# Two-layer decoder trunk on one core: moving operands placed elsewhere in the partition

## The chip, the cores and the metric

The kernel runs on one core of one Trainium2 chip. The metric is the device time of one execution in microseconds (us), the median of the runs shown. A core has a matrix engine (TensorE, PE in the profile, with its weight load PEld), a vector engine (VectorE, DVE), a scalar engine (ScalarE, ACT), GpSimd (POOL) and a queue engine that only issues transfers (SyncE, SP).

## The reference, cut to what matters

The input has 256 positions of width 1024, in float32. Layer 0 is: half-step SwiGLU, a Mamba-2 mixer, half-step SwiGLU. Then K and V are projected once from the stream. Layer 1 is: half-step SwiGLU, windowed attention over that K and V, half-step SwiGLU; a last RMSNorm ends it.

```python
def swiglu(h, w_gate, w_up, w_down):
    return (jax.nn.silu(h @ w_gate) * (h @ w_up)) @ w_down
...
        x = x + 0.5 * swiglu(rmsnorm(x, norm_w[layer, 0]), ...)      # 1024 -> 2816 -> 1024
        h = rmsnorm(x, norm_w[layer, 1])
        x = x + mamba2_mixer(h, ...)       # layer 0: 1024 -> 5152, scan, 2048 -> 1024
        x = x + swa_sink_attention(h, ...) # layer 1: 16 query heads, 4 key heads
        x = x + 0.5 * swiglu(rmsnorm(x, norm_w[layer, 2]), ...)
```

## The kernel before, in words

Everything is transposed: features lie on the 128 partitions, the 256 positions along them. The stream is eight tiles `X[k]` of 128 x 256. All weights come as 341 units of 128 x 1024 in one written-out order (`ORDER`), two units a transfer on SP's queue, into four buffers `raw`. To keep float32 accuracy each unit is split: ACT writes a rounded `hi` (L144), VectorE the rest `lo` (L155), each in a ring of six tiles of 4,096 bytes. An activation is split likewise, and a product is three matmuls: high by `hi`, low by `hi`, high by `lo`. Each matmul loads 128 x 128 of a weight unit (PEld) and streams the activation, the moving operand, past it.

There are two kinds of products.

- Products of the normed input. The input's parts stand joint in eight tiles `xs[k]` of 128 x 512: high in the first 256 columns, low in the other 256. Gate and up of a feed-forward go through `wide` (L351): for each k one matmul of 512 columns (`hi` by both parts) and one of 256 (`lo` by the high part); with `by_part` the eight of 512 come first and then the eight of 256. `by_part` holds in the two middle feed-forwards for all f but the first. The mixer's input projections and the queries go through `unit` (L336): 24 matmuls of 256 columns, from the same `xs`.
- The second products, through `rows` (L369): down projections (`da`, moving operands `hh`, `hl`), the mixer's output (`sa`, `yh`, `yl`) and the attention's output (`aa`, `oh`, `ol`). A unit is 24 matmuls of 256 columns: three for each of eight output tiles.

There are four feed-forwards of 22 steps f, each step a gate, an up and (four steps late, `LAG`) a down unit. The work between matmuls hangs on the units: after each one `tick` runs what is due in that slot (`Slots`) and splits weights ahead (`ahead`).

Memory of a partition is handed out in pools that stand in the order in which they are opened, each tile padded to 32 bytes. Before the change the order from below is: `const` (sm 2,048 bytes, co 1,024, `X` 8,192, `xs` 16,384, `ones` 512, three small tiles of 32, norms 256), `work` (8,384 in all), `raw` (32,768), `parts` (12 x 4,096: `hi`, then `lo`), and above them the pools of the stages, one after another at the same place (`ffn0`, `ssm`, then `kv` with `ffn1` and `att` above it, `ffn2`). The moving operands of the second products are in the stage's pool: `hh` and `hl` six tiles each, `yh` and `yl` six, `oh` and `ol` four. A tile of a ring is written again only when its last reader is done; a tile of a later pool waits for whatever had its bytes before.

Of the kernel before, what the change touches and what calls it, by code (L numbers as in the profile page):

```python
# [10 lines left out]
F32R = mybir.dt.float32r  # L11
# [5 lines left out]
P = 128  # L17
T = 256
D = 1024
KT = D // P  # L20
NF = 2816 // P
LAG = 4
# [87 lines left out]
class Weights:  # L110


    def __init__(self, nc, w, raw, parts):
        self.nc, self.w, self.raw, self.parts = nc, w, raw, parts
        self.loaded = 0
        self.cut = 0
        self.rounded = 0
        self.pos = 0
        self.chunks = {}
        self.ready = {}  # L120
# [95 lines left out]
class Trunk:  # L216
    def __init__(self, ctx, tc, a):
        self.ctx, self.tc, self.nc, self.a = ctx, tc, tc.nc, a
        nc = self.nc
        self.NPART = 6  # L220
        cp = self.cp = ctx.enter_context(tc.tile_pool(name="const", bufs=1))
        self.wk = ctx.enter_context(tc.tile_pool(name="work", bufs=2))
        raw = ctx.enter_context(tc.tile_pool(name="raw", bufs=RAW))
        parts = ctx.enter_context(tc.tile_pool(name="parts", bufs=self.NPART))
        self.ps = ctx.enter_context(tc.tile_pool(name="ps", bufs=4, space=PSUM))
        self.W = Weights(nc, a["w"], raw, parts)

        self.sm = cp.tile([P, NSM], F32, name="sm")
        self.co = cp.tile([P, NCO], F32, name="co")
        xp = [cp.tile([P, 2, T], F32, name=f"X{k}") for k in range(KT // 2)]  # L230
        self.X = [xp[k // 2][:, k % 2] for k in range(KT)]

        self.xs = [cp.tile([P, 2 * T], F32R, name=f"xs{k}") for k in range(KT)]
        self.xh = [x[:, 0:T] for x in self.xs]
        self.xl = [x[:, T:] for x in self.xs]
        self.ones = cp.tile([P, P], F32, name="ones")
        nc.vector.memset(self.ones, 1.0)
        self.mhalf = cp.tile([P, 2], F32, name="mhalf")
        nc.gpsimd.memset(self.mhalf, -0.5)
        self.eps = cp.tile([P, 1], F32, name="eps")  # L240
        nc.gpsimd.memset(self.eps, EPS)
        warm = cp.tile([P, 1], F32, name="warm")
        nc.scalar.activation(warm, self.ones[:, 0:1], AF.Silu)

        def first(t):
            q, h = nc.sync.dma_start, D // 2
            q(self.norms, a["norms"])
            q(xp[0], a["x"][:, 0:2, :])
            q(t[:, 0, :h], a["w"][0, :, 0, :h])
            q(xp[1], a["x"][:, 2:4, :])  # L250
            q(xp[2], a["x"][:, 4:6, :])
            q(t[:, 0, h:], a["w"][0, :, 0, h:])
            q(xp[3], a["x"][:, 6:8, :])
            for i in range(1, CH):
                q(t[:, i, :], a["w"][0, :, i, :])

        self.norms = cp.tile([P, NNO], F32, name="norms")
        self.W.load(first)
        self.W.load()
        nc.sync.dma_start(self.co, a["const"])  # L260
        self.W.load()
        nc.sync.dma_start(self.sm, a["small"])
        for _ in range(RAW - 3):
            self.W.load()
        self.ident = self.cc("ident")
        self.slots = Slots()
# [207 lines left out]
    def ffn(self, l, i, key, nxt):  # L474
        nc, wk = self.nc, self.fw
        self.stage_norm(key)
        accs = self.accs(f"da_{key}")
        hs = {}

        def evac(f, g, u):  # L480
            hh = wk.tile([P, T], F32R, tag="hh", bufs=LAG + 2, name=f"hh_{key}_{f}")
            hl = wk.tile([P, T], F32R, tag="hl", bufs=LAG + 2, name=f"hl_{key}_{f}")
            hs[f] = (hh, hl)

            def e0():
                nc.vector.tensor_tensor(g, g, self.rs, ALU.mult)
                nc.scalar.activation(g, g, AF.Silu)
                nc.vector.tensor_tensor(u, u, self.rs, ALU.mult)

            def e1():  # L490
                nc.vector.tensor_tensor(u, u, g, ALU.mult)
                nc.scalar.activation(hh, u, AF.Copy)

            def e2():
                nc.vector.tensor_tensor(hl, u, hh.bitcast(F32), ALU.subtract)

            wait = max(0, 4 - f) if key == "f0" else 2 if f == 0 else 0
            self.slots.chain(wait, [e0, e1, e2])

        def product(name, f, t):  # L500

            b = self.bank(f"{name}_{key}_{f}")
            if self.W.pos == 0:
                self.slots.at(0, lambda: nc.scalar.copy(t, b[:, 0:T]))
                self.unit((name, l, i, f), b[:, 0:T])
                return

            def add():
                nc.scalar.copy(t, b[:, T:])  # L509
                nc.vector.tensor_tensor(t, b[:, 0:T], t, ALU.add)  # L510

            self.slots.at(0, add)
            self.wide((name, l, i, f), b, by_part=l != i and f > 0)

        for f in range(NF):
            g, u = (wk.tile([P, T], F32, tag=n, bufs=4, name=f"{n}s_{key}_{f}") for n in "gu")
            product("g", f, g)
            evac_now = lambda: evac(f, g, u)
            self.slots.late(0, evac_now)
            product("u", f, u)  # L520
            if l == 1 and i == 0 and f == 0:
                self.split_k()
            if l == 1 and i == 0 and f == 5:
                self.shared_k()
            if f >= LAG:
                self.down(l, i, f - LAG, hs, accs)
        for f in range(NF - LAG, NF - 2):
            self.down(l, i, f, hs, accs)
        self.tail([(("d", l, i, f), *hs.pop(f)) for f in (NF - 2, NF - 1)], accs, nxt)
# [15 lines left out]
    def ssm(self, nxt):  # L545
        nc, tc, wk, sl = self.nc, self.tc, self.sw, self.slots
# [17 lines left out]
        B, C, xs, zs, CSB, CB, xdt, ys, M = ({} for _ in range(9))  # L564
        yh, yl, sq, R = {}, {}, {}, {}
# [188 lines left out]
        def ysplit(tt):  # L754
            y = ys[tt]
            w = self.s("snw", tt)
            h = yh[tt] = wk.tile([P, T], F32R, tag="yh", bufs=6, name=f"yh{tt}")
            l = yl[tt] = wk.tile([P, T], F32R, tag="yl", bufs=6, name=f"yl{tt}")
            sl.at(0, lambda: A.activation(h, y, AF.Copy, scale=w))
            sl.at(1, lambda: V.scalar_tensor_tensor(l, y, w, h.bitcast(F32), ALU.mult, ALU.subtract))  # L760

# [58 lines left out]
        for what in seq[:-2]:  # L820
            if what[0] == "so":
                tt = what[1]
# [79 lines left out]
    def att(self, nxt):  # L902
        nc, wk, sl = self.nc, self.aw, self.slots
        V, A = nc.vector, nc.scalar
        self.stage_norm("att")
        Q, S, SM_, PT, oh, ol = ({} for _ in range(6))
# [94 lines left out]
        def pv(j):  # L1001
            one = j < 3
            bs = [self.bank(f"pv{j}_{r}") for r in range(2 - one)]
            for kh in range(4):
                r, h = divmod(kh, 2)
                o = bs[r * (not one)][64 * h : 64 * h + 64, r * one * T : r * one * T + T]
                p = PT.pop((j, kh))
                v = slice(64 * kh, 64 * kh + 64)
                nc.tensor.matmul(o, self.V[:, 0, v], p[:, 0:2], start=True, stop=False, skip_group_check=True)
                nc.tensor.matmul(o[:, P:T], self.V[:, 1, v], p[:, 2], start=False, stop=True, skip_group_check=True)  # L1010
            for r in range(2):
                o = bs[r * (not one)][:, r * one * T : r * one * T + T]
                h = oh[j, r] = wk.tile([P, T], F32R, tag="oh", bufs=4, name=f"oh{j}_{r}")
                ol[j, r] = wk.tile([P, T], F32R, tag="ol", bufs=4, name=f"ol{j}_{r}")
                A.activation(h, o, AF.Copy)
            for r in range(2):
                o = bs[r * (not one)][:, r * one * T : r * one * T + T]
                V.tensor_tensor(ol[j, r], o, oh[j, r].bitcast(F32), ALU.subtract)
# [213 lines left out]
```

## Time and profile before

| | |
|---|---|
| median of 3 runs | 1062.36 us (1061.9 to 1063.26) |
| the profiled execution | 1063.96 us, its span 1062.2 us |
| mean granted TensorE clock | 0.994 |
| PE busy | 1040.4 us, 98% of the span |
| VectorE, ACT, POOL busy | 775.3, 627.5, 79.5 us |

The span runs from the first to the last profiled instruction. A matmul's row gives its start and a modelled duration of which a part overlaps the next one, so the pace of TensorE is read from start to start. A row of the timeline with "x8" stands for eight neighbours and gives the first one's start. PE means matmul, PEld weight load, L379 is line 379 of the kernel before.

### The profile page before, as it was taken

What the parts mean: (1) busy time and instruction counts of PE and PEld (TensorE: products, weight loads), DVE (VectorE), ACT (ScalarE), POOL (GpSimd) and SP (SyncE); (2) the same over time, 40 slices, a digit from 0 to 9 for tenths busy, and PEclk for the clock granted to TensorE, in tenths of its full rate; (3) what the DMA queues carried; (4) which work ended last, traced back from release to release, by engine and by line L of the source; (5) the groups of instructions that cost most, each with busy time, mean ns of one, the idle gap of its engine ahead of it and who ended that gap; (6) DMA issues with size and microseconds to landing.
All of it is one profiled execution on the core that took longest, in us unless ns stands there. A gap on an engine that the chain in (4) does not pass through costs nothing.

```text
span 1062.2 us, 18342 instructions
## 1 busy us (share of the span) xinstructions
PE 1040.4 (98%) x7290; PEld 961.3 (90%) x7290; DVE 775.3 (73%) x1420; ACT 627.5 (59%) x1106; POOL 79.5 (7%) x122
## 2 busy tenths in 40 slices
PE   8999999999999999999999999999999999999996
PEld 7899999999989898999999899999998898999996
DVE  4866666788999967766667796666689777666664
ACT  6555555579886756555555664555565765555554
POOL 3000000210111112000000200000022020000000
PEclk9999999999999999999999999999999999999998
DMA  8555455447545454545555465455544334545521
GB/s 303 202 186 198 165 197 185 174 176 273 182 149 211 160 180 165 193 168 196 188 192 189 148 216 187 170 194 192 197 170 160 110 145 173 198 172 193 191 100 40
DMA packets 30132, 190.84 MB, mean 180 GB/s; under 512 B 3904, under 2 KB 5728, under 8 KB 8544
## 3 DMA queue, kind: packets, MB, share of 16 engines
q1 hardware_dynamic: 30048, 189.69, 50.0%
q8 instruction: 57, 0.93, 0.4%
q14 instruction: 27, 0.22, 0.1%
HBM read 187.27 MB, written 1.10 MB: 177 GB/s over the span
## 4 chain that ended last, share of the span: by engine, by line
PE 81%; DVE 10%; ACT 4%; DMA 2%; POOL 1%; issue 1%; SPq 0%; ACTq 0%; DVEq 0%; POOLq 0%
PE da_f L379 23%; PE u_f L359 23%; PE g_f L359 22%; PE sa L379 4%; PE sb L346 3%; DVE lo L155 2%; PE aa L379 2%; PE q L346 1%; DMA csb<-cs_scratch 1%; DVE xs L598 1%; DVE xs L391 1%; ACT hi L144 1%; DVE E L720 1%; ACT E L715 1%; DMA raw<-w 1%
## 5 line engine op out<-in xcount | busy, mean ns | idle before, releaser
L155 DVE TENSOR_TENSOR lo<-raw,hi 128x1024 fp32r<-128x1024 f32 (+1 forms) x343 | 415.0, 1213 | 15.8 <-ACT hi L144 15.6
L144 ACT ACTIVATE hi<-raw 128x1024 fp32r<-128x1024 f32 (+1 forms) x343 | 357.4, 1047 | 22.3 <-PE da_f L379 6.2
L359 PE MATMUL u_f<-xs,hi 128*128 128x512 f32 x704 | 218.6, 398 | 0.0
L359 PE MATMUL g_f<-xs,hi 128*128 128x512 f32 x696 | 214.7, 397 | 0.6 <-DVE xs L391 0.4
L379 PE MATMUL da_f<-hh_f,hi 128*128 128x256 f32 x704 | 199.1, 283 | 0.0
L379 PE MATMUL da_f<-hl_f,hi 128*128 128x256 f32 x704 | 199.1, 283 | 0.0
L379 PE MATMUL da_f<-hh_f,lo 128*128 128x256 f32 x704 | 198.9, 283 | 0.0
L359 PEld LDWEIGHTS u_f<-xs,hi 128*128 128x128 f32 x704 | 129.8, 188 | 27.9
L359 PEld LDWEIGHTS g_f<-xs,hi 128*128 128x128 f32 x696 | 128.2, 189 | 27.4 <-DVE xs L391 1.5
L359 PE MATMUL u_f<-xs,lo 128*128 128x256 f32 x704 | 150.2, 281 | 0.0
L359 PE MATMUL g_f<-xs,lo 128*128 128x256 f32 x696 | 147.8, 281 | 0.0
L379 PEld LDWEIGHTS da_f<-hh_f,hi 128*128 128x128 f32 x704 | 134.5, 191 | 1.6
L379 PEld LDWEIGHTS da_f<-hh_f,lo 128*128 128x128 f32 x704 | 134.9, 192 | 0.0
L379 PEld LDWEIGHTS da_f<-hl_f,hi 128*128 128x128 f32 x704 | 134.8, 192 | 0.0
L510 DVE TENSOR_TENSOR gs_f<-g_f,gs_f 128x256 f32<-128x256 f32 x87 | 36.9, 424 | 121.9 <-ACT gs_f L509 121.9
L359 PEld LDWEIGHTS u_f<-xs,lo 128*128 128x128 f32 x704 | 116.0, 189 | 3.9
L359 PEld LDWEIGHTS g_f<-xs,lo 128*128 128x128 f32 x696 | 114.3, 189 | 3.8
L346 PE MATMUL sb<-xs,hi 128*128 128x256 f32 x656 | 107.8, 284 | 0.0
L510 DVE TENSOR_TENSOR us_f<-u_f,us_f 128x256 f32<-128x256 f32 x88 | 37.3, 423 | 91.1 <-ACT us_f L509 91.0
L509 ACT COPY us_f<-u_f 128x256 f32<-128x256 f32 x88 | 32.6, 371 | 113.1 <-PE u_f L359 113.1
L346 PEld LDWEIGHTS sb<-xs,hi 128*128 128x128 f32 x656 | 93.4, 188 | 1.1 <-issue 0.5
L509 ACT COPY gs_f<-g_f 128x256 f32<-128x256 f32 x87 | 32.1, 369 | 97.3 <-PE g_f L359 97.3
(252 smaller groups left out, 1376.7 us busy)
## 6 DMA issues: line engine op xcount, KB each, us to landing
raw<-w SPq DMA_DIRECT2D x168, 1024.0 KB, 4.9
csb<-cs_scratch SPq DMA_DIRECT2D x8, 768.0 KB, 7.0
raw<-w SPq DMA_DIRECT2D x4, 512.0 KB, 7.9
X<-x SPq DMA_DIRECT2D x4, 256.0 KB, 5.7
Q<-r_q SPq DMA_DIRECT2D x32, 32.0 KB, 1.9
out<-o SPq DMA_DIRECT2D x3, 256.0 KB, 2.2
ca<-const_att SPq DMA_DIRECT2D x1, 704.0 KB, 4.1
raw<-w SPq DMA_DIRECT2D x2, 256.0 KB, 5.7
```

The source lines that it names most:

```text
L144: self.nc.scalar.activation(hi[:, s], self.chunks[c][:, i, s], AF.Copy)
L155: self.nc.vector.tensor_tensor(lo[:, s], self.chunks[c][:, i, s], hi[:, s].bitcast(F32), ALU.subtract)
L346: nc.tensor.matmul(out, w[:, k * P : (k + 1) * P], x[k], start=n == 0, stop=n == len(passes) - 1)
L359: self.nc.tensor.matmul(out[:, 0:c], w[:, k * P : (k + 1) * P], x[k], start=n == 0, stop=n == len(passes) - 1, skip_group_check=True,)
L379: nc.tensor.matmul(out, w[:, s], x, start=f and j < 4 and m == 0, stop=e and m == 2, skip_group_check=True)
L391: nc.vector.scalar_tensor_tensor(self.xl[j], self.X[j], wcol(j), self.xh[j].bitcast(F32), ALU.mult, ALU.subtract)
L509: nc.scalar.copy(t, b[:, T:])
L510: nc.vector.tensor_tensor(t, b[:, 0:T], t, ALU.add)
L598: V.scalar_tensor_tensor(out, u[:, tap : tap + T], self.s("convw", tap * 24 + c), out, ALU.mult, ALU.add)
L715: A.activation(e, e, AF.Exp, scale=-1.0)
L720: V.tensor_tensor(f, f, c, ALU.mult)
```

## The change: two kinds of tiles move, three rings become one

The eight `xs` tiles leave `const` for a pool of their own, opened with `side="right"`: it is handed out from the end of the partition downwards. The parts of the second products' operands leave the stages' pools for one pool `op` that stands between `const` and `work` for the whole kernel, with two rings (`high`, `low`) of six tiles of 1,024 bytes. `hh`, `yh` and `oh` take turns in the first, `hl`, `yl` and `ol` in the second. No instruction is added, removed or reordered in the program's text. `work`, `raw` and `parts` come to stand 4,096 bytes lower.

```diff
         cp = self.cp = ctx.enter_context(tc.tile_pool(name="const", bufs=1))
+        self.op = ctx.enter_context(tc.tile_pool(name="op", bufs=LAG + 2))
+        top = ctx.enter_context(tc.tile_pool(name="top", bufs=1, side="right"))
         self.wk = ctx.enter_context(tc.tile_pool(name="work", bufs=2))
...
-        self.xs = [cp.tile([P, 2 * T], F32R, name=f"xs{k}") for k in range(KT)]
+        self.xs = [top.tile([P, 2 * T], F32R, name=f"xs{k}") for k in range(KT)]
...
-            hh = wk.tile([P, T], F32R, tag="hh", bufs=LAG + 2, name=f"hh_{key}_{f}")
-            hl = wk.tile([P, T], F32R, tag="hl", bufs=LAG + 2, name=f"hl_{key}_{f}")
+            hh = self.op.tile([P, T], F32R, tag="high", name=f"hh_{key}_{f}")
+            hl = self.op.tile([P, T], F32R, tag="low", name=f"hl_{key}_{f}")
...
-            h = yh[tt] = wk.tile([P, T], F32R, tag="yh", bufs=6, name=f"yh{tt}")
-            l = yl[tt] = wk.tile([P, T], F32R, tag="yl", bufs=6, name=f"yl{tt}")
+            h = yh[tt] = self.op.tile([P, T], F32R, tag="high", name=f"yh{tt}")
+            l = yl[tt] = self.op.tile([P, T], F32R, tag="low", name=f"yl{tt}")
...
-                h = oh[j, r] = wk.tile([P, T], F32R, tag="oh", bufs=4, name=f"oh{j}_{r}")
-                ol[j, r] = wk.tile([P, T], F32R, tag="ol", bufs=4, name=f"ol{j}_{r}")
+                h = oh[j, r] = self.op.tile([P, T], F32R, tag="high", name=f"oh{j}_{r}")
+                ol[j, r] = self.op.tile([P, T], F32R, tag="low", name=f"ol{j}_{r}")
```

## Rows read from the trace of the kernel before

**Rows 1.** The page, part 1: busy us (share of the span) xinstructions
```profile
PE 1040.4 (98%) x7290; PEld 961.3 (90%) x7290; DVE 775.3 (73%) x1420; ACT 627.5 (59%) x1106; POOL 79.5 (7%) x122
```

**Rows 2.** Waits of PE: engine line waited for: us, times, longest us
```profile
PE st_yg L331 <- DVE dg_yg L326: 4.8, 4, 2.0
PE g_f L346 <- ACT hi L144: 1.5, 2, 0.9
PE st_yg L306 <- POOL ss_yq L296: 1.1, 1, 1.1
...
PE s L916 <- DVE m L931: 0.2, 1, 0.2
```

**Rows 3.** Groups by line and shape: xcount | busy us, mean ns
```profile
L359 PE MATMUL u_f<-xs,hi 128*128 128x512 f32 x704 | 218.6, 398 | 0.0
...
L379 PE MATMUL da_f<-hh_f,hi 128*128 128x256 f32 x704 | 199.1, 283 | 0.0
...
L346 PE MATMUL sb<-xs,hi 128*128 128x256 f32 x656 | 107.8, 284 | 0.0
...
L379 PE MATMUL sa<-yh,hi 128*128 128x256 f32 x128 | 37.7, 295 | 0.0
...
L346 PE MATMUL q<-xs,hi 128*128 128x256 f32 x128 | 23.6, 285 | 0.0
...
L379 PE MATMUL aa<-oh,hi 128*128 128x256 f32 x64 | 18.5, 289 | 0.0
```

**Rows 4.** Timeline of PE: a down unit (start, modelled us, what), first, last, next
```profile
162.09 0.28 PE L379 MATMUL da_f<-hh_f,hi 128*128 128x256 f32 x1
...
164.84 0.28 PE L379 MATMUL da_f<-hl_f,hi 128*128 128x256 f32 x1
164.97 0.40 PE L359 MATMUL g_f<-xs,hi 128*128 128x512 f32 x1
```

**Rows 5.** Timeline of PE: the shared key's second unit and the next
```profile
631.33 0.28 PE L346 MATMUL kab<-xkh,hi 128*128 128x256 f32 x1
...
634.21 0.28 PE L379 MATMUL da_f<-hh_f,hi 128*128 128x256 f32 x1
```

**Rows 6.** Timeline of PE: mixer input units, 69 matmuls from first to last row
```profile
221.38 0.28 PE L346 MATMUL sb<-xs,lo 128*128 128x256 f32 x1
...
229.54 0.28 PE L346 MATMUL sb<-xs,lo 128*128 128x256 f32 x1
```

**Rows 7.** Timeline of PE: a gate unit of eight pairs, start of the next
```profile
31.41 0.40 PE L359 MATMUL g_f<-xs,hi 128*128 128x512 f32 x1
31.65 0.28 PE L359 MATMUL g_f<-xs,lo 128*128 128x256 f32 x1
31.77 0.39 PE L359 MATMUL g_f<-xs,hi 128*128 128x512 f32 x1
...
34.23 0.40 PE L359 MATMUL u_f<-xs,hi 128*128 128x512 f32 x1
```

**Rows 8.** Timeline of PE: seven pairs of an earlier up unit
```profile
22.02 0.39 PE L359 MATMUL u_f<-xs,hi 128*128 128x512 f32 x1
22.25 0.28 PE L359 MATMUL u_f<-xs,lo 128*128 128x256 f32 x1
...
24.45 0.39 PE L359 MATMUL g_f<-xs,hi 128*128 128x512 f32 x1
```

**Rows 9.** Timeline of PE: a gate unit with the wide matmuls first
```profile
434.08 2.02 PE L359 MATMUL g_f<-xs,hi 128*128 128x512 f32 x8
435.95 1.11 PE L359 MATMUL g_f<-xs,lo 128*128 128x256 f32 x8
436.90 2.02 PE L359 MATMUL u_f<-xs,hi 128*128 128x512 f32 x8
```

**Rows 10.** All waits: those of the writers of the second products' operands
```profile
ACT hh_f L492 <- DVE us_f L491: 40.9, 85, 1.3
...
ACT oh L1015 <- PE pv L1010: 2.8, 4, 1.2
```

**Rows 11.** Windows: length, busy PE, PEld, DVE, ACT, POOL, granted clock, DMA
```profile
202.00:401.30 199.30, 193.38 (x1606) 187.22 (x1606) 173.50 (x332) 146.22 (x261) 29.99 (x52) 0.99 0.51 186
401.30:590.00 188.70, 188.55 (x1244) 172.52 (x1243) 130.69 (x218) 104.02 (x172) 7.13 (x12) 1.00 0.53 188
590.00:784.60 194.60, 194.44 (x1293) 178.43 (x1292) 139.02 (x234) 108.94 (x183) 9.82 (x14) 1.00 0.52 186
```

## The prediction, made before the result was known

> **What bounds the kernel now.** The page's first part comes first: PE is busy 98% of the span, and no other engine comes near [rows 1]. The list of PE's waits says whether it ever stands still for data: eleven entries, all small, the largest 4.8 us in four times [rows 2]. The windows by stage say the same: in the two middle feed-forwards PE is busy for all but 0.15 us of 188.7 and 0.16 of 194.6, at a granted clock of 1.00, the upper level of 2.4 GHz; only the mixer leaves 5.9 us of 199.3 [rows 11]. So the end is set by the pace at which matmuls follow one another. The list of groups gives the counts [rows 3], the timeline the pace, from start to start.
>
> Read it in five places. A down unit takes from 162.09 to 164.97, 2.88 us for 24 matmuls of 256 columns: 120.0 ns each [rows 4]. The shared key's second unit takes 2.88 us as well, 120.0 ns [rows 5]. The mixer's input units, of the same shape, run 69 matmuls in 8.16 us: 118.3 ns each [rows 6]. A gate unit of eight pairs (512 and 256 columns) takes 2.82 us, 353 ns a pair [rows 7], but earlier the same form ran seven pairs in 2.43 us, 347 ns [rows 8]. With the wide ones first it is 1.87 us for the eight of 512 and 0.95 for the eight of 256, again 2.82 [rows 9]. So one shape has two paces, 120.0 and 118.3, and one pair has two, 353 and 347, with no engine in the way. The key's unit goes through the same function as the mixer's and differs in where its moving operand lies: it stands among the late pools, not in `const`. That is what the change touches.
>
> **Where the operands lie.** The pools' sizes give the distances. Before, from the first `xs` tile to the first `hi` tile are 16,384 + 512 + 96 + 256 (rest of `const`) + 8,384 (`work`) + 32,768 (`raw`) = 58,400 bytes, which is 32 more than a multiple of 256. `xs` tiles are 2,048 bytes and weight slices 512, so every matmul on `xs` reads moving data that stand 32 bytes short of its weights, modulo 256. `hh`, `hl`, `oh`, `ol`, `yh`, `yl` and the key's operands stand at 0 modulo 256 from the weights (sums of multiples of 256). The first kind has the pace of 118.3, the second 120.0, at low and high places alike. After, `op` stands below `work`: from its tiles to the weights are multiples of 1,024 plus 8,384 plus 32,768, so they stand 64 past the weights modulo 256; and if the end of the partition's usable room is at 229,344 bytes, as the allocator's limit reads, `xs` also stands 64 past. Both kinds get one distance, and it is one that no row of the kernel before shows. The key's operands keep theirs.
>
> **The parts and their costs.** All counts from [rows 3].
>
> *Second products, moved below the weights.* 704 x 3 down, 128 x 3 mixer output, 64 x 3 attention output: 2,688 matmuls, now at 120.0 ns [rows 4]. Nearest rows for another distance: 118.3 [rows 6]. I take it: 2,688 x 1.7 ns = 4.5 us less. Bounds: the fast pair leaves 347 - 230 = 117 ns for its 256 columns [rows 8], so 2,688 x 3 = 8.1 us less; on the other side nothing shows over 120 for a whole unit, and I allow the same 1.7 ns, 4.5 us more.
>
> *Interleaved gate and up.* All units of the first and last feed-forward and four at the start of the middle ones, less the very first: 91 units, 728 pairs at 353 ns [rows 7]. Value 0, because either pace was met at one distance. Bounds: 347 [rows 8], 728 x 6.7 = 4.9 us less; and every pair like the slow one of [rows 7], 0.36 us, 4.9 us more.
>
> *Gate and up with the wide ones first.* 84 units [rows 9]. Value 0. Bounds: eight at 230 ns and eight at 117 make 2.78 us, 0.04 less, 3.7 us in all; eight at 240 (the first step of [rows 7]) and eight at 120 make 2.88, 0.06 more, 5.0 us in all.
>
> *Input products of 256 columns.* 41 mixer units and 8 of queries, 1,176 matmuls at 118.3 [rows 6]. Value 0; at 117 it is 1.5 us less, at 120 2.0 us more.
>
> *One ring for three.* `hh` and `yh` had six tiles and have six; `oh` had four. At a seam of stages the first tile to be overwritten is the one six back, whose matmuls ended units ago. `oh`'s writer waits today for its own product alone, 2.8 us in four times, `hh`'s for VectorE's product of gate and up [rows 10]; neither waits for a buffer, so more room gives nothing. Behind these writers on ACT stand the weights' `hi`, and PE would wait for those; since PE's whole wait for `hi` is 1.5 us [rows 2], cover is there and the price is 0. Transfers, ACT and VectorE work keep their number and order; their covers stay.
>
> The sum is 4.5 us less: 1063.96 becomes 1059.5 for the profiled execution, which lies 1.6 us above the median; the median 1062.4 becomes 1057.9. All lower bounds together would be 18.2 us less, all upper ones 16.4 more.
>
> **A rule against it.** The same matmul has 120.0 and 118.3 ns by where its moving operand lies [rows 5, 6]. The Trainium skill, SBUF — State Buffer, section "Who interferes with whom", says that PE never waits on anyone, and TensorE: Matmul & The Clock Gate, section "Step-by-step: what each phase is for", that loading the next weights takes no read bandwidth from the running matmul. By that no placement would matter and the time would stay 1062.4; the two paces speak against it, though two paces at one distance [rows 7, 8] leave room for causes other than place. It is the rival "nothing" below.
>
> **Rivals.**
>
> *Slower: both kinds fall into the pace of 120.* The two distances seen differ also by where a moving operand starts within 64 bytes: weights, `hh` and the key stand at 32, `xs` at 0. After the change both moving kinds stand at 32. If that start decides and not the distance, the second products keep 120.0 and the input products take it: 1,176 x 1.7 = 2.0 us, and the eight of 256 in 84 units go from 0.95 to 0.96, 0.9 us: 3 us more, 1065.4. If the 512 ones go to 240 ns as well, it adds up to 9 us, 1074. It decides if the 256-column step on `xs` reads 120.0. For it: 120.0 held in every place that has that start. Against it: these all have the same distance too, so the rows can't part the two.
>
> *Faster by more: gate and up stay in the pace of 347.* 4.9 us besides the 4.5: 1053. For it: the pace was held over seven pairs [rows 8]. Against it: it was met once, early, and lost.
>
> *Nothing.* Moved bytes cost nothing: 1062.4. For it: two paces at one distance [rows 7, 8], so what sets them may be a phase that the place does not touch. Against it: 120.0 and 118.3 never changed sides in the units that I read [rows 4 to 6].
>
> *A new wait at a seam.* The joint ring could hold a stage's first `yh` or `oh` back. The slot's last reader is six tiles back, so I give it a price of under 1 us and little chance.
>
> **How the numbers follow.** Chances: forecast 0.35 (1057.9, its own range 1055 to 1060), faster by more 0.09, nothing 0.19, slower at the pace of 120 0.34, new wait 0.03. A change within 0.2%, 2.1 us, can't be told from none here. Faster: 0.35 + 0.09, 0.43 after rounding off some of the forecast into the bound; same 0.19 and a small part of the slower case, 0.21; slower 0.36 with the wait. The range takes in the slower case up to half of its second step and the faster one with part of the lower bounds: 1050 to 1069.
>
> **What would show it.** In the profile after, the start-to-start step of a down unit tells the first term: 118.3 or less if right, 120.0 if the start within 64 bytes decides. The step of a mixer input unit tells the slower rival: 120.0 there and it is right. The key's second unit is the control, 120.0 either way. The pairs of the last feed-forward show 353, 347 or 360. PE's list of waits must stay as short as it is. The prediction is wrong if the down units stay at 120.0, or if the 512-column steps move, for which I have put no change.

## The result: 1.3% faster, most of it in the two middle feed-forwards

| | before | after |
|---|---|---|
| median of the runs made side by side | 1062.81 us (1061.9 to 1063.5) | 1048.99 us (1047.58 to 1050.46) |
| ratio, 95% interval | | 0.9871 [0.9854, 0.9888] |
| span of the profiled execution | 1062.2 us | 1046.9 us |
| mean granted clock | 0.994 | 0.993 |

The gain is 13.8 us, where 4.5 was forecast. The first part of the page answers to [rows 1]:

```profile
PE 1025.2 (98%) x7290; PEld 948.2 (91%) x7290; DVE 775.1 (74%) x1420; ACT 627.7 (60%) x1106; POOL 79.4 (8%) x122
```

The same 7,290 matmuls, PE still busy 98%, but 15.2 us shorter; the weight loads take 13.1 us less, VectorE, ACT and POOL what they did. The list of PE's waits (total us, times, longest) answers to [rows 2]; it has thirteen entries against eleven and 11.6 us in all against 11.4:

```profile
PE st_yg L334 <- DVE dg_yg L329: 3.4, 3, 1.8
PE st_yg L309 <- POOL ss_yq L299: 1.2, 1, 1.2
PE warm L1066 <- DVE ones L240: 1.0, 1, 1.0
...
PE g_f L349 <- ACT hi L144: 0.9, 1, 0.9
```

So matmuls follow one another faster. The windows, cut at the first matmul of each stage (columns as in [rows 11]: stretch, length, busy PE, PEld, DVE, ACT, POOL, granted clock, DMA share, GB/s), say where:

```profile
0.00:201.70 201.70, 197.49 (x1287) 180.15 (x1287) 135.15 (x225) 113.18 (x190) 11.42 (x21) 0.99 0.58 206
201.70:398.54 196.84, 192.17 (x1606) 185.88 (x1605) 173.45 (x332) 146.24 (x260) 29.95 (x52) 0.99 0.53 191
398.54:770.70 372.16, 371.65 (x2534) 341.77 (x2533) 269.16 (x451) 212.84 (x353) 16.82 (x24) 1.00 0.54 191
770.70:1046.80 276.10, 263.92 (x1870) 240.38 (x1868) 197.38 (x415) 155.41 (x306) 21.25 (x28) 0.99 0.42 147
```

The two middle feed-forwards (third row) took 188.7 + 194.6 = 383.3 us before [rows 11] and take 372.2 now: 11.1 of the 15.3 us that the span lost, at a granted clock of 1.00, the 2.4 GHz level, in both. The mixer lost 2.5 (199.3 to 196.8). The first feed-forward, and the last together with the attention, lost the rest, under 2. The change moved operands in all of them alike, so the stages differ in something else.

The timeline of PE, from start to start. A down unit of the first feed-forward, first row, last row and the next unit's first, answers to [rows 4]:

```profile
162.11 0.28 PE L382 MATMUL da_f<-hh_f,hi 128*128 128x256 f32 x1
...
164.82 0.28 PE L382 MATMUL da_f<-hl_f,hi 128*128 128x256 f32 x1
164.94 0.40 PE L362 MATMUL g_f<-xs,hi 128*128 128x512 f32 x1
```

2.83 us for 24 matmuls: 117.9 ns, from 120.0. The interleaved gate unit ahead of it answers to [rows 7], 2.82 us, as before:

```profile
156.46 0.40 PE L362 MATMUL g_f<-xs,hi 128*128 128x512 f32 x1
...
159.28 0.40 PE L362 MATMUL u_f<-xs,hi 128*128 128x512 f32 x1
```

A whole step of a middle feed-forward (down, gate, up, next down) answers to [rows 9]:

```profile
436.27 0.28 PE L382 MATMUL da_f<-hh_f,hi 128*128 128x256 f32 x1
...
438.99 1.99 PE L362 MATMUL g_f<-xs,hi 128*128 128x512 f32 x8
440.82 1.11 PE L362 MATMUL g_f<-xs,lo 128*128 128x256 f32 x8
441.76 2.00 PE L362 MATMUL u_f<-xs,hi 128*128 128x512 f32 x8
443.60 1.07 PE L362 MATMUL u_f<-xs,lo 128*128 128x256 f32 x8
444.50 0.28 PE L382 MATMUL da_f<-hh_f,hi 128*128 128x256 f32 x1
```

The down unit takes 2.72 us, 113.3 ns a matmul; gate takes 1.83 + 0.94 = 2.77, up 1.84 + 0.90 = 2.74, where both took 2.82. Up's eight narrow matmuls run at 0.90 / 8 = 113 ns and the down unit behind them runs on at that pace.

The control, the shared key's second unit with the unit behind it, answers to [rows 5]:

```profile
622.37 0.28 PE L349 MATMUL kab<-xkh,hi 128*128 128x256 f32 x1
...
625.25 0.28 PE L382 MATMUL da_f<-hh_f,hi 128*128 128x256 f32 x1
...
628.08 2.00 PE L362 MATMUL g_f<-xs,hi 128*128 128x512 f32 x8
```

The key's unit takes 2.88 us, 120.0 ns, as it did. The down unit behind it is one of a middle feed-forward, with the same operands and the same order as its neighbours at 113.3, and takes 2.83 us: 117.9 ns. It differs from them in the unit ahead; the unit behind it is a wide-first gate, as behind them.

The mixer's input units, the same 69 matmuls as [rows 6]:

```profile
221.05 0.28 PE L349 MATMUL sb<-xs,lo 128*128 128x256 f32 x1
...
229.17 0.28 PE L349 MATMUL sb<-xs,lo 128*128 128x256 f32 x1
```

8.12 us, 117.7 ns, from 118.3.

### The profile page after: what moved, and what is told of

The parts are those of the page before. It is cut to its first block, busy times and chain, and to the rows that moved or that the text cites. A ratio compares the mean times of both kernels' runs of the same rounds, so it can differ in the third digit from the quotient of the medians.

```text
span 1046.9 us, 18340 instructions
## 1 busy us (share of the span) xinstructions
PE 1025.2 (98%) x7290; PEld 948.2 (91%) x7290; DVE 775.1 (74%) x1420; ACT 627.7 (60%) x1106; POOL 79.4 (8%) x122
## 4 chain that ended last, share of the span: by engine, by line
PE 80%; DVE 11%; ACT 3%; DMA 2%; POOL 1%; issue 1%; SPq 0%; ACTq 0%; DVEq 0%; POOLq 0%
PE u_f L362 23%; PE g_f L362 22%; PE da_f L382 22%; PE sa L382 3%; PE sb L349 3%; DVE lo L155 2%; DVE xs L394 2%; DMA csb<-cs_scratch 2%; PE aa L382 1%; PE q L349 1%; DVE xs L601 1%; DVE X L402 1%; DMA raw<-w 1%; DVE E L723 1%; ACT hi L144 1%
## 5 line engine op out<-in xcount | busy, mean ns | idle before, releaser
L382 PE MATMUL da_f<-hh_f,hi 128*128 128x256 f32 x704 | 195.8, 278 | 0.0
L382 PE MATMUL da_f<-hh_f,lo 128*128 128x256 f32 x704 | 195.6, 278 | 0.0
L382 PE MATMUL da_f<-hl_f,hi 128*128 128x256 f32 x704 | 195.6, 278 | 0.0
L382 PEld LDWEIGHTS da_f<-hh_f,hi 128*128 128x128 f32 x704 | 132.3, 188 | 1.7
L382 PEld LDWEIGHTS da_f<-hl_f,hi 128*128 128x128 f32 x704 | 132.2, 188 | 0.0
L382 PEld LDWEIGHTS da_f<-hh_f,lo 128*128 128x128 f32 x704 | 132.1, 188 | 0.0
```

The lines of the kernel that those rows point to most:

```text
L382: nc.tensor.matmul(out, w[:, s], x, start=f and j < 4 and m == 0, stop=e and m == 2, skip_group_check=True)
```

## The experiments

Steps below are means from start to start over the whole trace of a run, steps over 150 ns (260 for 512 columns), which hold a wait or a low clock, left out. "Distance" is from the weights to the moving operand, modulo 256 bytes: for `xs` 224 (32 short) before and 64 after, for the second products 0 and 64.

**The two halves alone.** E1 moves `xs` only, E2 moves the second products only.

Against the changed kernel, E1 (`hl`, `yh`, `yl`, `oh` and `ol` go back in the same way) and then E2:

```diff
-        self.op = ctx.enter_context(tc.tile_pool(name="op", bufs=LAG + 2))
...
-            hh = self.op.tile([P, T], F32R, tag="high", name=f"hh_{key}_{f}")
+            hh = wk.tile([P, T], F32R, tag="hh", bufs=LAG + 2, name=f"hh_{key}_{f}")
```
```diff
-        self.xs = [top.tile([P, 2 * T], F32R, name=f"xs{k}") for k in range(KT)]
+        self.xs = [cp.tile([P, 2 * T], F32R, name=f"xs{k}") for k in range(KT)]
```

> Only the normed input's tiles go to the far end (64 bytes past the weights modulo 256); the second products' operands stay in the stages' pools (distance 0). If each kind of product keeps its own pace, the down units stay at 120.0 ns a matmul and only gate, up and the input products gain what they gained in the whole change (3.0 us in gate and up, 0.7 in the mixer's input): about 1059 us, 3.7 less than before. Rival, that the pace is carried over from one unit to the next: the down units fall below 120.0 as well, or gate and up gain less than 3 us.

> Only the second products' operands go to the pool below the weights (distance 64); the normed input stays where it was (32 short). If each kind keeps its own pace: down 115.6, mixer output 117.8, attention output 115.0 ns a matmul, 11.4 us less, about 1051 us; gate and up as before, 233.7 and 118.7 ns. Rival, the pace is carried over: the down units of the middle feed-forwards don't reach their fast pace of 113 without the new gate and up, stay near 117.8, and about 6 us are gained, 1056.

E1: 1058.7 us, 0.9958 [0.9942, 0.9975]; down stays at 119.8 ns. E2: 1057.51 us, 0.9943 [0.9926, 0.996]; down falls to 117.75 and stays there in the middle feed-forwards too, as a down unit in E2's timeline shows (first row, next unit's first):

```profile
437.18 0.28 PE L381 MATMUL da_f<-hh_f,hi 128*128 128x256 f32 x1
...
440.00 2.02 PE L361 MATMUL g_f<-xs,hi 128*128 128x512 f32 x8
```

2.82 us against 2.72 in the full change. So 113.3 needs `xs` moved as well, though a down unit doesn't read `xs`. E1 came out as paces of their own would have it, E2 as the rival, a pace that is carried over, would: that speaks against taking units one by one.

**Place or distance.** E3 leaves all tiles in the old pools and puts pads of 96 bytes ahead of `xs`, 160 behind them and 64 ahead of the stages' pools, which makes both distances 64. E4 keeps the new pools and pads them back to the old distances. E3 against the kernel before, then E4 against the changed one:

```diff
+        self.pad_a = cp.tile([P, 24], F32, name="pad_a")
         self.xs = [cp.tile([P, 2 * T], F32R, name=f"xs{k}") for k in range(KT)]
...
+        self.pad_b = cp.tile([P, 40], F32, name="pad_b")
...
+        self.pad_c = late.tile([P, 16], F32, name="pad_c")
```
```diff
+        self.pad_a = low.tile([P, 48], F32, name="pad_a")
         self.op = ctx.enter_context(tc.tile_pool(name="op", bufs=LAG + 2))
+        self.pad_b = mid.tile([P, 16], F32, name="pad_b")
...
+        self.pad_t = end.tile([P, 24], F32, name="pad_t")
         self.xs = [top.tile([P, 2 * T], F32R, name=f"xs{k}") for k in range(KT)]
```

> The kernel before with unused bytes put in: 96 ahead of the normed input's tiles, 160 behind them, 64 ahead of the stages' pools. All tiles keep their old places to within 320 bytes, but both kinds of moving operand, and the key's, stand 64 bytes past the weights modulo 256, as in the changed kernel. Distance theory: the time of the changed kernel, 1049 us, with the same steps (down 115.6, 512-column 231), and the key's unit below 120.0 too. Place theory (the far end, or below the weights, is what counts): 1062.5, all steps as before.

> The changed kernel with unused bytes put in so that the old distances come back: second products at 0, normed input 32 short, the tiles otherwise at their new places. Distance theory: the time of the kernel before, 1062.5 us, down units at 120.0 ns. Place theory: 1049 us, down units at 115.6.

E3: 1048.16 us, 0.986 [0.9843, 0.9877], down at 115.58 ns on the mean, as after the change (115.64). E4: 1062.83 us, 1.0 [0.999, 1.0009], down at 119.79. The far end of the partition, the pool below the weights and the joint ring count nothing; the distance counts for all of it.

E3 moves the key's operands to 64 as well, and its second unit and the down unit behind it answer, as was expected of the key:

```profile
622.08 0.28 PE L350 MATMUL kab<-xkh,hi 128*128 128x256 f32 x1
...
624.80 0.28 PE L383 MATMUL da_f<-hh_f,hi 128*128 128x256 f32 x1
...
627.52 1.99 PE L363 MATMUL g_f<-xs,hi 128*128 128x512 f32 x8
```

Both take 2.72 us, 113.3 ns, where the changed kernel, with its key at 0, has 2.88 and 2.83. The down unit has the same distance in both; the key's unit ahead of it has not.

**The distance itself.** The changed kernel with the three pads of E4 in other widths (columns of `pad_a`, `pad_b`, `pad_t`), so that both distances are the one named: 128 (16, 48, 48), 192 (32, 32, 32), 32 (56, 8, 8), 96 (8, 56, 56), 0 (48, 16, 16), 160 (24, 40, 40) and 224 (40, 24, 24). E12 keeps both at 64 and moves every start by 32 bytes (8, none, 56).

> Both kinds of moving operand 128 bytes past the weights modulo 256, at the new places. If the pattern repeats every 128 bytes (or 64), 128 is the same as 0, which the second products had before: the down units are at 120.0 ns a matmul. If it repeats every 256 only, they have a pace of their own, 113 to 118, or more.

> Both 192 bytes past the weights modulo 256. If the pattern repeats every 128 bytes this is the changed kernel's distance of 64: 1049 us, down units at 115.6 ns. If it repeats every 64, it would equal 0 as well, which the changed kernel has refuted. If every 256 only, another time.

> Both 32 past. No distance near it was seen. If being near the weights' phase is what costs, this is slow like distance 0: down at 120 ns, 1063 us or more. If every distance but 0 is free of the 120.0, below 1058.

> Both 96 past. If the pattern repeats every 128 bytes, this is the same as 32 short, the distance that the normed input had before: the input units keep their 118.3 ns, gate and up pairs 353, and the down units go to about 118.3 too: about 1058 us. If it repeats every 256 only, another time.

> Both kinds at distance 0. The down units stay at 120.0 ns a matmul. If the distance alone sets the pace, the input's 256-column matmuls, until now at 118.3, take 120.0 as well: at least 2 us more than before, 1065 us. Rival, that the two kinds differ by something else than distance: they stay at 118.3 and the time is 1062.5.

> Both 160 past, the last distance with no run near it. If neighbours are alike (128 gave 1058, 192 gave 1050), something between; if the pace jumps from one multiple of 32 to the next (64 fast, 96 slow, 128 between), anything from 1047 to 1064.

> Both 224 past, which is the 32 short that the normed input had before. Distance alone: the input's matmuls as before (118.3 ns, 512 columns at 233.7), the down units at the same 118.3 instead of 120.0: about 3.5 to 4.5 us less than before, 1058 us, which is the term that the prediction summed.

> The changed kernel with everything from the pool of second products' operands upwards and the normed input moved by 32 bytes: both distances stay 64, but moving operands and weights start at 0 instead of 32 within 64 bytes. Distance alone: 1049 us and the steps of the changed kernel. If where a stream starts within 64 bytes counts as well, the steps differ: anything up to 1062.

| both distances | median us | ratio, 95% interval | down ns | up, 512 ns | up, 256 ns | mixer input ns |
|---|---|---|---|---|---|---|
| before (224; 0) | 1062.81 | 1 | 119.79 | 233.69 | 118.62 | 118.30 |
| E9: 0 | 1060.95 | 0.9986 [0.9977, 0.9996] | 119.97 | 232.67 | 117.87 | 119.82 |
| E7: 32 | 1050.38 | 0.9892 [0.9875, 0.9908] | 116.93 | 230.80 | 117.85 | 116.75 |
| the change: 64 | 1048.99 | 0.9871 [0.9854, 0.9888] | 115.64 | 231.38 | 116.70 | 117.56 |
| E8: 96 | 1062.35 | 1.0 [0.999, 1.0009] | 119.95 | 232.98 | 118.75 | 119.87 |
| E5: 128 | 1058.34 | 0.9964 [0.9951, 0.9977] | 119.35 | 231.2 | 119.31 | 118.86 |
| E10: 160 | 1053.29 | 0.992 [0.9906, 0.9935] | 117.68 | 231.57 | 117.71 | 118.22 |
| E6: 192 | 1049.89 | 0.9886 [0.9871, 0.9901] | 115.55 | 233.82 | 116.31 | 115.41 |
| E11: 224 | 1058.45 | 0.9966 [0.9948, 0.9983] | 118.33 | 232.4 | 118.5 | 118.27 |
| E12: 64, other start | 1049.74 | 0.9884 [0.9866, 0.9902] | 115.64 | 231.33 | 116.71 | 117.36 |

Down units of the middle feed-forwards at 192 (E6) and 96 (E8), first row and the next unit's first:

```profile
436.89 0.28 PE L388 MATMUL da_f<-hh_f,hi 128*128 128x256 f32 x1
...
439.61 2.02 PE L368 MATMUL g_f<-xs,hi 128*128 128x512 f32 x8
```
```profile
437.48 0.28 PE L388 MATMUL da_f<-hh_f,hi 128*128 128x256 f32 x1
...
440.36 2.03 PE L368 MATMUL g_f<-xs,hi 128*128 128x512 f32 x8
```

2.72 us against 2.88: 113.3 and 120.0 ns for the same work. One distance is not best for all shapes: 192 is best for the mixer's input (115.41) and worst for 512 columns (233.82); 32 is best for 512 columns (230.80) and second for the mixer's input (116.75). These means mix both orders of gate and up and hold for the orders of the changed kernel. E9 was expected at 1065 us if the distance alone counts: the mixer's input did go to 119.82, but the steps of gate and up fell by 0.7 to 1.0 ns, and the time came out below that of before. Distances 128 apart (64 and 192, 32 and 160) don't agree, so 128 bytes are not the period; E3 and E12, whose distances differ from the changed kernel's by multiples of 256 or whose starts differ, have the pace of 64. E12 settles the rival on the start within 64 bytes: it moved the start from 32 to 0, and the down units stayed at 115.64. E11's eight runs spread from 1055.22 to 1061.83 us, more than any other kernel's here; its steps are those of the run of 1056.64.

**The unit ahead.** What is left is why the middle feed-forwards gain 11.1 us and the outer ones, with the attention, under 2. They differ in the order of gate and up (`by_part`) and in the order of the three passes of down (`high_first`). E13 puts the first everywhere, E14 the second, E15 both; E16 puts both into the kernel before. The first edit, then the second:

```diff
-            self.wide((name, l, i, f), b, by_part=l != i and f > 0)
+            self.wide((name, l, i, f), b, by_part=f > 0)
```
```diff
-        self.rows([(hi_lo, hh, hl)], accs, f == 0, False, high_first=l != i)
+        self.rows([(hi_lo, hh, hl)], accs, f == 0, False, high_first=True)
```

> The changed kernel, with the 84 gate and up units of the two outer feed-forwards (all but each one's first column) in wide-first order too; the down units keep their order. In the trace of the changed kernel an interleaved unit takes about 2,822 to 2,832 ns, a wide-first up unit 2,741 and a wide-first gate unit 2,772. Theory A (a down unit runs on at the pace that the unit ahead of it settled in): gate and up lose about 42 x 0.085 + 42 x 0.055 = 5.9 us, and the outer feed-forwards' down units, at about 117.8 ns a matmul now, run at about 113.3, which is 42 x 24 x 4.5 ns = 4.5 us more: about 1,038.6 us. Rival B (a down unit's pace is its own pass order's): only the 5.9 us, 1,043 us, and the outer down units stay at 117.8. Rival C (the order counts nothing): 1,049.

> The changed kernel, with the passes of the down units in all four feed-forwards in the order of the middle ones (both products of the high weights first). Rival B (own pass order): the outer down units fall from 117.8 to 113.3 ns a matmul, 4.5 us, so about 1,044.5 us. Theory A (the unit ahead sets it): the outer down units follow interleaved units as before and stay near 117.8: 1,049 us within 1 us.

> Both orders in all four feed-forwards of the changed kernel. Theory A and rival B alike: the outer feed-forwards run as the middle ones do, gate and up 5.9 us and down 4.5 us less, about 1,038.6 us. If the first alone gives this too, the pass order of the down units counts nothing.

> The same two orders in the kernel before, with its old distances. If the order gains only together with the new distances: the wide-first units took 2,813 ns there against 2,826 for the interleaved, so 84 x 0.013 = 1.1 us, and at most 1 us in the down units: 1,060.5 to 1,062 us. If the order gains by itself: some 10 us, 1,052.

| | median us | ratio, 95% interval | outer down unit us | outer gate, up us |
|---|---|---|---|---|
| the change | 1048.99 | 0.9871 [0.9854, 0.9888] | 2.83 | 2.82 to 2.83 |
| E13 wide first | 1039.22 | 0.9782 [0.9768, 0.9797] | 2.72 | 2.77, 2.74 |
| E14 high first | 1048.38 | 0.9869 [0.9855, 0.9884] | 2.83 | 2.82 to 2.83 |
| E15 both | 1038.56 | 0.9781 [0.9766, 0.9796] | 2.72 | 2.77, 2.74 |
| E16 both, old distances | 1061.31 | 0.9992 [0.9982, 1.0001] | 2.87 | 2.81 |

The first feed-forward in E13, to be held against the rows at 162.11 above:

```profile
157.49 0.28 PE L382 MATMUL da_f<-hh_f,hi 128*128 128x256 f32 x1
...
160.21 1.99 PE L362 MATMUL g_f<-xs,hi 128*128 128x512 f32 x8
162.03 1.11 PE L362 MATMUL g_f<-xs,lo 128*128 128x256 f32 x8
162.98 2.00 PE L362 MATMUL u_f<-xs,hi 128*128 128x512 f32 x8
164.81 1.07 PE L362 MATMUL u_f<-xs,lo 128*128 128x256 f32 x8
165.72 0.28 PE L382 MATMUL da_f<-hh_f,hi 128*128 128x256 f32 x1
```

E13 didn't touch the down units, and they fell from 2.83 to 2.72 us. E14 changed their own order, and they stayed (162.38 to 165.21):

```profile
162.38 0.28 PE L382 MATMUL da_f<-hh_f,hi 128*128 128x256 f32 x1
...
165.21 0.40 PE L362 MATMUL g_f<-xs,hi 128*128 128x512 f32 x1
```

So what goes ahead decides which pace a down unit settles in. At the old distances the order doesn't do this: in E16 it brings 0.9 us, not separable from nothing. Nor is wide first the better order at every distance: at 32 (E7) settled interleaved gate and up units take 2.77 us, wide-first ones 2.81. E13 was expected at 1,038.6 and came out a little above; its windows by stage show the sum:

```profile
0.00:195.78 195.78, 192.56 (x1286) 176.96 (x1287) 134.70 (x225) 113.02 (x190) 11.33 (x20) 0.99 0.60 212
195.78:394.60 198.82, 193.54 (x1606) 187.37 (x1605) 173.65 (x332) 146.43 (x260) 30.11 (x53) 0.98 0.53 190
...
766.84:1037.70 270.86, 258.54 (x1870) 236.47 (x1868) 197.12 (x415) 155.43 (x306) 21.29 (x28) 0.99 0.44 150
```

The first feed-forward lost 5.9 us and the last stretch 5.2, and the mixer, which was not touched, took 2.0 more in this execution (198.8 against 196.8). E13 and E15 beat both kernels: some 10 us less than the change, some 23 less than before.

The order ahead is not all that is handed on. In the second middle feed-forward of E7 (both distances 32), here is the down unit of the step before the shared key's units, then that of the first step behind theirs. Both stand behind wide-first units:

```profile
611.57 0.28 PE L388 MATMUL da_f<-hh_f,hi 128*128 128x256 f32 x1
...
614.37 2.03 PE L368 MATMUL g_f<-xs,hi 128*128 128x512 f32 x8
...
634.18 0.28 PE L388 MATMUL da_f<-hh_f,hi 128*128 128x256 f32 x1
...
637.01 2.03 PE L368 MATMUL g_f<-xs,hi 128*128 128x512 f32 x8
```

They take 2.80 and 2.83 us, and the down units behind the second keep 2.83 to the end of the stage, where the whole feed-forward ahead had 2.80. In E10 (160) the pace changes at the same place the other way, from 2.85 to 2.82. The attention's last units, behind the same `pv` matmuls at distance 64, have two paces as well, in the changed kernel (first pair of rows, start of one unit and of the next) and in E14, which altered nothing there:

```profile
838.36 0.28 PE L382 MATMUL aa<-oh,hi 128*128 128x256 f32 x1
...
841.08 0.28 PE L382 MATMUL aa<-oh,hi 128*128 128x256 f32 x1
```
```profile
838.59 0.28 PE L382 MATMUL aa<-oh,hi 128*128 128x256 f32 x1
...
841.42 0.28 PE L382 MATMUL aa<-oh,hi 128*128 128x256 f32 x1
```

2.72 and 2.83 us; E12 and E13 have the first, E3 and E15 the second. So at one distance and in one order more than one pace can last, and other units in between can change it. What picks the pace there is not shown.

## Why the prediction was wrong on the size

**Reading of the bound: right.** Pace of TensorE, no other engine, waits of 11.4 and 11.6 us in all; the one ring in place of three cost nothing (E3, with three, has 1048.16), and no wait for its tiles stands in PE's list.

**Distance decides: right, and shown** by E3 and E4. The byte counts give 64 for the second products by the pool sizes alone. For `xs` they also need where the pools begin, which the prediction doesn't give; that it is 64 is borne out by E3, whose distances lie between neighbouring pools and whose up units have the changed kernel's 512-column step (231.28 and 231.38 ns).

**Second products, 4.5 us: mis-sized.** The step was to take 118.3 from the nearest row [rows 6] and 117 as the lower bound. The change in the means gives for down 2,112 x (119.79 - 115.64) = 8.8 us, for the mixer's output (119.83 to 117.80) 384 x 2.0 = 0.8, for the attention's (119.80 to 114.96) 192 x 4.8 = 0.9: 10.5 in all, beyond the bound of 8.1. The attention's part is not sure: at the same distance E14 and E15 have 117.25 and 117.24. The value of 118.3 belongs to the old `xs` distance: E11, with both kinds there, has 118.33. It says nothing of 64. No row of before could show 113.3. That the sign came out right is in part luck: 118.3 was carried over to a distance without a row, and at 96 the down units have 119.95 (E8).

**Wide first, 0: wrong, outside its bounds.** Over the 44 steps of the middle feed-forwards (42 of them wide first) the mean gate unit fell from 2.833 to 2.800 us and up from 2.825 to 2.757: 4.4 us, where 3.7 was the lower bound. Down there fell from 2.875 to 2.723, 6.7 us. The two make the 11.1 of the windows. **Interleaved, 0: held** (2.827 us in the outer feed-forwards, before and after). **Input products, 0: nearly**, 984 x 0.74 + 192 x 0.94 ns = 0.9 us.

**The step that failed** stands under these terms: each unit's pace was taken as its own, so a down unit could not depend on `xs`, and 0 was written wherever a new distance met a shape without a row. E2 against the change (117.75 and 115.64), the unit behind the key's, in the changed kernel and in E3, and E13 against E14 show that the pace is handed on from unit to unit. In the middle feed-forwards both parts of the change are needed: by the mean units, E1 takes 1.5 us off them and E2 2.2, the two together 11.1. So two terms were wrong: the second products gave 10.5 us and not 4.5, and gate and up with the wide ones first gave 4.4 and not 0.

**The rivals.** "Both kinds fall into the pace of 120" did not happen here, and its reason, the start within 64 bytes, fell with E12. The pace itself exists: at 96 (E8) down and the mixer's input both stand at 119.9, and there the time is that of before (1.0 [0.999, 1.0009]), not 3 us more; the 1,400 steps of 512 columns, 0.7 ns shorter, give 1.0 us of it back, and the rest is not accounted for. "Nothing" is excluded by the interval. "Pairs at 347" was not seen in the settled units of the changed kernel, but the pace can last: in E11, with `xs` at the old distance, a pair takes 347 ns all through the first feed-forward (2.77 us a unit) and 353 in the last. The Trainium skill, SBUF — State Buffer, section "Who interferes with whom", has PE never wait on anyone, and TensorE: Matmul & The Clock Gate, section "Step-by-step: what each phase is for", has the next weight load take no read bandwidth. If placement counts nothing by them, as the prediction read them, they don't agree with 113.3 and 120.0 ns for one matmul form by the distance between its two operands, and the measurement decides. Whether a read port has to do with it no run shows.

**Open:** what in the chip makes the distance count, what the unit ahead hands on, and what picks one of two lasting paces at one distance and order (E7, E10, the attention's output). The runs vary distance and order only; no row shows the cause under them.

## What to carry to other kernels

Where TensorE is busy all the time, take its pace from start to start, unit by unit, and compare equal matmuls in different surroundings before you call a pace the form's own. If two paces of one form show up, a pad of some bytes between moving operand and weights is a cheap thing to sweep, all distances modulo 256 and every shape, and the order within the unit ahead is to be tried together with it: neither the order alone (0.9992) nor the distance alone (0.9871) gave what both did (0.9781). Which order is better is to be tried at each distance. A shape at a distance that no row shows has no price; zero is a guess with a width, and terms may not be added where one unit sets the pace of the next.

## What the chip showed that was not expected

- A float32r matmul of 256 columns in a settled down unit takes 113.3 to 120.0 ns, one of 512 on the mean of a trace 229 (E13) to 234 (E6), by the distance modulo 256 bytes between its operands and by the order. The granted clock of the middle feed-forwards was 1.00 throughout.
- At one distance there are several steady paces. At 64 a down unit holds 113.3 ns behind wide-first units and 117.9 behind interleaved ones or a key's unit at 0, over its 24 matmuls. In E7 the key's two units change the down units behind them from 2.80 to 2.83 us for the rest of the stage.
- Distances are not symmetric: 32 and 224 gave 0.9892 and 0.9966.
